# Both MLP products of a hybrid decoder layer by one level of Strassen

## The chip, the cores and the metric

The kernel runs on one core of a Trainium2 chip. The metric is the device time of one execution in microseconds (us): the median of the runs shown, lower is better. The core has five engines that matter here: TensorE (PE; its weight loads are listed apart as PEld), VectorE (DVE), ScalarE (ACT), GpSimd (POOL) and SyncE (SP), which issues most transfers. Matrix products read SBUF and write to PSUM.

## What is computed

One decoder layer over 512 tokens of 1024 features, all in float32: a gated merge of a convolution branch and a latent attention branch, a cross-attention to 256 memory tokens, an MLP and a last RMS norm. The change is in the MLP and in what feeds and follows it:

```
u = rms_norm(h, norm_mlp_g)                               # h: 512 x 1024
h = h + square(relu(u @ w_mlp1)) @ w_mlp2                 # 1024 x 4096, 4096 x 1024
return rms_norm(h, final_norm_g)
```

The two MLP products are of 512 x 1024 x 4096 multiplications each.

## The kernel before

Every float32 product runs as three passes over operands that are split into a high part (rounded to float32r, 12 significant bits) and a low part (the rest): `mm3` (lines 228 to 235) issues high x high, high x low and low x high into one PSUM bank. So each operand is first split: ACT casts the high part (line 199), and DVE or POOL subtracts it from the source for the low part (line 200, `split`; its last argument chooses the engine).

Activations are kept feature-major: feature on the partitions, 512 tokens on the free side. In a product the weights are the stationary operand (128 x 128 each) and 512 tokens move past them, so a product instruction is 128x512.

Weights lie in HBM in the order of use, in chunks of mostly 1 MB (`_stream`, line 97). `raw` (line 291) loads them from SP's queue into two buffers, one chunk ahead. `prep` (line 313) splits 1024 columns of a chunk at a time into `wh` and `wl` (three buffers each, `whl`, line 308). `Pipe.unit` (line 337) emits the splits of one unit ahead of the products of the unit before it, so that TensorE finds its weights ready. TensorE's order is that of emission; the order on the other engines is chosen by the scheduler of the framework, near the order of emission.

`w_eng` (line 321) names the engine of the low parts of the weights. In most of the first half it is POOL (line 627), while DVE runs the convolution with its running sum in PSUM. From the output projection of the cross-attention on (line 1131) it is DVE, and POOL has nothing to do until the end.

The stages that the change touches, in order:

- `xo_unit` (line 1119): the output projection of the cross-attention, in four units of two feature blocks. Behind each block `Norm.add` (line 963) adds the product to the residual `ht`, scales it by the norm's gain, splits it into `hgh` and `hgl`, and adds up its squares.
- The first MLP product, `m1_unit` (line 1151), 32 blocks of 128 hidden features in two halves of 16, each a sum over 8 blocks of input features (24 product instructions). `evac_m1` (line 1142) applies the norm's factor, relu and square and splits the result into `hh` and `hl_`.
- The second MLP product, `m2_unit` (line 1163): behind each half of the hidden features, 8 blocks of output features, each a sum over 16 hidden blocks, added to `ht`. In the second half the squares of the final norm are added up beside it.
- The last output block goes by halves of 256 tokens (lines 1189 to 1263), so that the final norm of the first half of the tokens runs beside the products of the second; then eight blocks are scaled and stored, feature-major; the host transposes the result.

Of the kernel before, what the change touches and what calls it, by code (L numbers as in the profile page):

```python
# [14 lines left out]
F32 = mybir.dt.float32  # L15
# [77 lines left out]
# gate chunks that come before the key/value latents  # L93
# [3 lines left out]
def _stream():  # L97
    """The weight chunks in the order of use: key, matrix, first row, row blocks, columns."""
# [34 lines left out]
    for h in range(2):  # L133
        for i in range(8):
            out.append((("m1", h, i), "w_mlp1", 0, 8, r(2048 * h + 256 * i, 256)))
        for i in range(8):
            out.append((("m2", h, i), "w_mlp2", 16 * h, 16, r(128 * i, 128)))
    return out


def _pack(arrays):
    """All weight chunks, each [partition, row block, column], one after the other."""
    parts = []
    for _, name, k0, kt, cols in _stream():
# [21 lines left out]
def _body(tc, a):  # L166
# [30 lines left out]
    # ---------------------------------------------------------------- exact splits and products  # L197
# [8 lines left out]
    # PE issues in the order of emission; small products that wait for other engines are put off  # L206
    # by a number of ticks (a tick: three passes over 512 columns)
# [20 lines left out]
    def mm3(out, pairs, first=True, last=True):  # L228
        n = len(pairs)
        cols = out.shape[-1] / S  # L230
        for i, ((wh, wl), (ah, al)) in enumerate(pairs):
            pe.matmul(out, wh, ah, start=first and i == 0, stop=False)  # L232
            pe.matmul(out, wh, al, start=False, stop=False)  # L233
            pe.matmul(out, wl, ah, start=False, stop=last and i == n - 1)  # L234
            tick(cols)
# [11 lines left out]
    # ---------------------------------------------------------------- constants  # L247
# [31 lines left out]
    # ---------------------------------------------------------------- weight stream  # L279
    stream = _stream()  # L280
    ch, offs = {}, []
    o = 0
    for i, (key, _, _, kt, cols) in enumerate(stream):
        ch[key] = i
        offs.append(o)
        o += P * kt * len(cols)
# [26 lines left out]
    def prep(key, k0=0, kt=None, c0=0, cols=128):  # L313
        """hi/lo of rows blocks k0.. and columns c0.. of a chunk, as [P, kt, cols]."""
# [11 lines left out]
    class Pipe:  # L326
        """splits the weights of one unit ahead of the unit before it."""
# [22 lines left out]
    # ================================================================ scopes of the first half  # L350
# [34 lines left out]
    # ---------------------------------------------------------------- x * g, split  # L385
    # the tables of the scalar engine and the clock of the PE array come up while the first loads run
# [34 lines left out]
    # ---------------------------------------------------------------- rotary tables  # L421
# [50 lines left out]
    # ---------------------------------------------------------------- background conv work  # L472
# [14 lines left out]
    def conv_gen():  # L487
        # two channel tiles in turn, so that no step waits for the one before it
# [16 lines left out]
    def layer_norm_in():  # L505
        # token-major
# [47 lines left out]
    # ---------------------------------------------------------------- w_in  # L554
# [41 lines left out]
    # first pair of channel tiles: both products follow the arriving row blocks of x  # L596
# [39 lines left out]
    # latent projections, token-major: [token, column]  # L636
# [94 lines left out]
    # ================================================================ MLA  # L731
# [148 lines left out]
    # ================================================================ merge and w_out  # L880
# [73 lines left out]
    class Norm:  # L954
        """h += psum; h * g, split; the sums of squares of h's rows."""
# [63 lines left out]
    # ================================================================ memory cross-attention  # L1019
# [3 lines left out]
    xoh = xa.tile([P, XH, S], F32R, name="xoh")  # L1023
    xol = xa.tile([P, XH, S], F32R, name="xol")
# [92 lines left out]
    n2 = Norm(hgp, "norm_mlp_g", hgh, hgl)  # L1117
# [12 lines left out]

    w_eng[0] = dve
    for m2 in range(4):
        xo_unit(m2)
    pipe.ahead(lambda: prep(("m1", 0, 0)))
    close(xa_cm, xm_cm)

    # ================================================================ MLP
    ml_cm, mlp = pool("mlp", side="right")
    hh = mlp.tile([P, 16, S], F32R, name="hh")
    hl_ = mlp.tile([P, 16, S], F32R, name="hl")  # L1140

    def evac_m1(b, m):
        t = mlp.tile([P, S], F32, tag="mz", name="mz", bufs=2)
        dve.scalar_tensor_tensor(t, b, 0.0, n2.rb, op0=ALU.max, op1=ALU.mult)  # L1144
        s = mlp.tile([P, S], F32, tag="ms", name="ms", bufs=2)
        act.activation(s, t, AF.Square)
        if m == 0:
            act.activation(warm, s[:, 0:1], AF.Sqrt)
        split(hh[:, m, :], hl_[:, m, :], s)

    def m1_unit(half, m):
        def main(hl):
            b = bank()
            mm3(b, hg_pairs(hl))
            n2.then(lambda: evac_m1(b, m))
        pipe.unit(lambda: prep(("m1", half, m // 2), c0=128 * (m % 2)), main)

    fin = mlp.tile([P, S], F32, name="fin")
    eps = mlp.tile([P, 1], F32, name="eps")
    gps.memset(eps, EPS)  # L1160
    mb_ = {}

    def m2_unit(half, m, q):
        def main(hl):
            if q == 0:
                mb_[0] = bank()
            b = mb_[0]
            mm3(b, [(lhs(hl, k), (hh[:, 8 * q + k, :], hl_[:, 8 * q + k, :])) for k in range(8)],
                first=q == 0, last=q == 1)
            if q == 1:  # L1170
                dve.tensor_tensor(ht[:, m, :], ht[:, m, :], b, op=ALU.add)
                if half == 1:
                    if m == 0:
                        act.activation(fin, ht[:, m, :], AF.Square)
                    else:
# [6 lines left out]
    for half in range(2):  # L1182
        for m in range(16):
            m1_unit(half, m)
# [104 lines left out]
```

## Time and profile before

| | us |
|---|---|
| median of 3 runs | 813.68 |
| lowest and highest | 813.56, 814.76 |
| the profiled execution: span from first to last instruction | 811.6 |
| TensorE busy in it (97% of the span) | 783.2 |
| VectorE busy (61%) | 495.9 |
| ScalarE busy (43%) | 346.4 |
| GpSimd busy (20%) | 158.6 |

The profile is of one execution; 2.1 us of the median lie outside its span. Rows of a timeline give the start, the recorded duration, the engine, the line, the operation, what is written from what is read, the shapes and the count of the instructions merged into the row; a bracket tells how long the engine had been idle and who ended that. Durations of matrix products overlap, so their pace is read from their starts. The recorded time of an instruction includes time in which it has been issued and is held. In a windows view each engine has its busy time and its number of instructions in the stretch, then follow the granted clock of TensorE (1.00 is 2.4 GHz, 0.50 is 1.2 GHz), the share of the DMA engines and GB/s.

### The profile page before, as it was taken

Reading aid. Unit: us, or ns where it says so; the run is one execution under the profiler, and the core shown is the slowest. Engines: PE = TensorE matmul, PEld = TensorE weight load, DVE = VectorE, ACT = ScalarE, POOL = GpSimd, SP = SyncE. Lnnn points to the kernel's source line nnn. Section 1 sums busy time; section 2 is a strip of 40 time slices with the busy share of each in tenths; the row PEclk is TensorE's granted clock in tenths of the full one; section 3 lists DMA queues with packets and bytes.
Section 4 is the critical chain, followed back from the end, with each engine's and each line's share of the span. In section 5 each row is a group of like instructions: output and inputs, shape, how many; then the busy total and the mean of one; then the engine's idle time right before and its main releaser. Section 6 shows DMA issues by size and latency. Waiting matters only on the chain.

```text
span 811.6 us, 9532 instructions
## 1 busy us (share of the span) xinstructions
PE 783.2 (97%) x3730; PEld 647.3 (80%) x3730; DVE 495.9 (61%) x781; ACT 346.4 (43%) x585; POOL 158.6 (20%) x92
## 2 busy tenths in 40 slices
PE   8799999999999998998999999999999999999995
PEld 4589788778788886888878888888888888888885
DVE  5898999734888869766787654443233444533333
ACT  7323334478666546343475354332212434432321
POOL 4444436322321304445320000000000000000001
PEclk9999999999999998999999999999999999999998
DMA  8213124122103242232321322222332222222203
GB/s 274 95 45 124 55 82 156 62 81 92 53 1 105 98 162 104 103 105 104 105 104 52 105 104 104 86 79 96 103 104 104 104 96 76 89 103 104 104 0 104
DMA packets 18492, 77.67 MB, mean 96 GB/s; under 512 B 1680, under 2 KB 7184, under 8 KB 11024
## 3 DMA queue, kind: packets, MB, share of 16 engines
q1 hardware_dynamic: 15120, 72.00, 25.6%
q10 hardware_dynamic: 3328, 5.07, 1.8%
q8 instruction: 29, 0.48, 0.2%
q14 instruction: 15, 0.12, 0.1%
HBM read 74.97 MB, written 2.10 MB: 95 GB/s over the span
## 4 chain that ended last, share of the span: by engine, by line
PE 75%; DVE 18%; ACT 3%; issue 3%; DMA 1%; SPq 0%; DVEq 0%; ACTq 0%
PE mm L234 23%; PE mm L232 23%; PE mm L233 23%; DVE cv L483 6%; DVE q L200 1%; DVE mt L906 1%; DVE rs_t L243 1%; DMA xr<-xT 1%; PE at L799 1%; DVE sg L710 1%; PE at L778 1%; PE at L780 1%; ACT wh L199 1%; PE at L781 0%; DVE mt L905 0%
## 5 line engine op out<-in xcount | busy, mean ns | idle before, releaser
L199 ACT CAST wh<-raw 128x1024 fp32r<-128x1024 f32 (+4 forms) x135 | 136.5, 1012 | 321.5 <-PE mm L233 279.7
L200 POOL TENSOR_TENSOR wl<-raw,wh 128x1024 fp32r<-128x1024 f32 (+4 forms) x65 | 144.6, 2227 | 255.2 <-ACT wh L199 248.1
L200 DVE TENSOR_TENSOR wl<-raw,wh 128x1024 fp32r<-128x1024 f32 x70 | 85.7, 1224 | 73.3 <-ACT wh L199 73.3
L232 PE MATMUL mm<-hgh,wh 128*128 128x512 f32 x288 | 113.0, 392 | 0.0
L234 PE MATMUL mm<-hgh,wl 128*128 128x512 f32 x288 | 112.8, 392 | 0.0
L233 PE MATMUL mm<-hgl,wh 128*128 128x512 f32 x288 | 112.6, 391 | 0.0
L232 PE MATMUL mm<-hh,wh 128*128 128x512 f32 (+1 forms) x272 | 102.6, 377 | 0.0
L233 PE MATMUL mm<-hl,wh 128*128 128x512 f32 (+1 forms) x272 | 102.4, 376 | 0.0
L234 PE MATMUL mm<-hh,wl 128*128 128x512 f32 (+1 forms) x272 | 102.4, 376 | 0.0
L483 DVE SCALAR_TENSOR_TENSOR cv<-zpad,vec,cv 128x512 f32<-128x512 f32 x116 | 80.0, 744 | 0.1
L1245 POOL TENSOR_TENSOR ht<-ht,rbf 128x256 f32<-128x256 f32 x4 | 2.9, 736 | 384.1 <-ACT rbf L1237 384.1
L232 PE MATMUL mm<-uh,wh 128*128 128x512 f32 x176 | 71.3, 405 | 1.8 <-DVE sg L710 1.8
L1144 DVE SCALAR_TENSOR_TENSOR mz<-mm,rb 128x512 f32<-128x512 f32 x32 | 22.0, 691 | 79.7 <-PE mm L234 78.7
L234 PE MATMUL mm<-uh,wl 128*128 128x512 f32 x176 | 69.8, 397 | 0.5 <-DVE wl L200 0.5
L233 PE MATMUL mm<-ul,wh 128*128 128x512 f32 x176 | 69.9, 397 | 0.0
L234 PEld LDWEIGHTS mm<-hgh,wl 128*128 128x128 f32 x288 | 54.3, 189 | 11.5
L233 PEld LDWEIGHTS mm<-hgl,wh 128*128 128x128 f32 x288 | 54.5, 189 | 11.2
L232 PEld LDWEIGHTS mm<-hgh,wh 128*128 128x128 f32 x288 | 54.5, 189 | 11.2
L234 PEld LDWEIGHTS mm<-hh,wl 128*128 128x128 f32 x272 | 51.2, 188 | 9.4
L232 PEld LDWEIGHTS mm<-hh,wh 128*128 128x128 f32 x272 | 51.2, 188 | 9.4
L233 PEld LDWEIGHTS mm<-hl,wh 128*128 128x128 f32 x272 | 51.2, 188 | 9.3
L232 PEld LDWEIGHTS mm<-uh,wh 128*128 128x128 f32 x176 | 33.3, 189 | 11.1 <-issue 3.8
(327 smaller groups left out, 1407.1 us busy)
## 6 DMA issues: line engine op xcount, KB each, us to landing
raw<-weights SPq DMA_DIRECT2D x58, 1024.0 KB, 4.8
raw<-weights SPq DMA_DIRECT2D x4, 768.0 KB, 4.2
xr<-xT SPq DMA_DIRECT2D x8, 256.0 KB, 6.2
raw<-weights SPq DMA_DIRECT2D x4, 512.0 KB, 5.1
ht<-xT ACTq DMA_DIRECT2D x1, 2048.0 KB, 9.4
raw<-weights SPq DMA_DIRECT2D x2, 576.0 KB, 3.4
mr<-memT ACTq DMA_DIRECT2D x1, 1024.0 KB, 5.8
mtok<-mem ACTq DMA_DIRECT2D x1, 1024.0 KB, 7.9
```

The costliest lines, as they stand in the source:

```text
L199: act.copy(hi, src)
L200: (eng or dve).tensor_tensor(lo, src, hi.bitcast(F32), op=ALU.subtract)
L232: pe.matmul(out, wh, ah, start=first and i == 0, stop=False)
L233: pe.matmul(out, wh, al, start=False, stop=False)
L234: pe.matmul(out, wl, ah, start=False, stop=last and i == n - 1)
L243: dve.scalar_tensor_tensor(t, dst, -0.5, dst, op0=ALU.mult, op1=ALU.mult)
L483: dve.scalar_tensor_tensor(run if w < CW - 1 else acc[:, c, :], zs, wcol, run, op0=ALU.mult, op1=ALU.add)
L710: dve.tensor_tensor(t, b, rbx, op=ALU.mult)
L778: pe.matmul(b[:, :n], q[:, 0, sl], k[:, 0, :n], start=True, stop=False)
L780: pe.matmul(b[:, :n], q[:, 0, sl], k[:, 1, :n], start=False, stop=False)
L799: pe.transpose(b[:, (t - k) * P:(t - k + 1) * P], ptok[h, t][:, k * P:(k + 1) * P], ident)
L1144: dve.scalar_tensor_tensor(t, b, 0.0, n2.rb, op0=ALU.max, op1=ALU.mult)
```

## The change

Both matrices of a product are halved in each direction, and seven products of half-size blocks (the Winograd form of Strassen's scheme) take the place of eight. Sums and differences of blocks are made before and after.

**The first product** stays feature-major. The tokens are halved (256 each), so its product instructions are 128x256. A unit is two neighbouring blocks of hidden features (16 units, 7 block products of 4 x 3 instructions each). The blocks of the activations and their four combinations are made once, in `NormS.add`, in the place of `Norm.add`, partly on POOL. The combinations of the weights are made in each unit (`prep_m1`): five on POOL, in place, and four splits of 512 or 1024 elements on ACT and DVE. The norm's factor is no longer applied here: squared, it moves behind the second product (`r2`). Hidden features are kept unsplit (`hid`). PSUM banks of a unit are accumulated again after they have been read (`again=True`).

**The second product** is token-major: hidden tokens are the stationary operand, and 512 columns of the weights move (128x512). It runs in six passes over the four chunks of a block of the weights, the third pass with two products per chunk. Each chunk splits 1024 hidden values (`split_h`, DVE for the low part) and 2048 weights (`split_w`, the low part in two POOL instructions), behind the sums that it needs (`sums_of`, `x_minus`, DVE). Blocks of the weights that are needed again are loaded again: 24 chunks instead of 16.

**The residual** is transposed by TensorE and written to HBM during the first product (`spill`), and read back token-major from ACT's queue where a result is finished (`residual`). The final norm works on rows of tokens, so that the transposes and broadcasts of the old ending go, and the output is stored token-major. A fourth buffer pair for split weights (`whl4`) is added.

The diff, cut to its core:

```diff
-    for h in range(2):
-        for i in range(8):
-            out.append((("m1", h, i), "w_mlp1", 0, 8, r(2048 * h + 256 * i, 256)))
-        for i in range(8):
-            out.append((("m2", h, i), "w_mlp2", 16 * h, 16, r(128 * i, 128)))
+    for i in range(16):
+        out.append((("m1", i), "w_mlp1", 0, 8, r(256 * i, 256)))
+    for p, (j, l) in enumerate(M2_READS):
+        for c in range(4):
+            out.append((("m2", p, c), "w_mlp2", 16 * j + 4 * c, 4, r(512 * l, 512)))
...
+        def add(self, m, b):
+            dve.tensor_tensor(ht[:, m, :], ht[:, m, :], b, op=ALU.add)
+            u = n2p.tile([P, S], F32, tag="u", name="u", bufs=2)
+            act.activation(u, ht[:, m, :], AF.Copy, scale=v_("norm_mlp_g", m))
+            j = m % 4
+            if m < 4:
+                dve.tensor_tensor(t1f[:, j, :], u[:, HT:], u[:, :HT], op=ALU.subtract)
+                split(b11[0][:, j, :], b11[1][:, j, :], u[:, :HT])
+                split(t1_[0][:, j, :], t1_[1][:, j, :], t1f[:, j, :])
+                gps.tensor_copy(u12[:, j, :], u[:, HT:])
+            else:
+                t = n2p.tile([P, 3, HT], F32, tag="hA" if m % 2 else "hB", name="t", bufs=2)
+                dve.tensor_tensor(t[:, 0, :], u[:, HT:], t1f[:, j, :], op=ALU.subtract)
+                gps.tensor_tensor(t[:, 1, :], u[:, HT:], u12[:, j, :], op=ALU.subtract)
+                dve.tensor_tensor(t[:, 2, :], u[:, :HT], t[:, 0, :], op=ALU.subtract)
+                split(b2_[0][:, j, :], b2_[1][:, j, :], u)
+                split(t234[0][:, j], t234[1][:, j], t)
...
+                gps.tensor_tensor(self.acc, self.acc, q, op=ALU.add)
...
+    def prep_m1(i):
+        r = raw("m1", i)
+        a11, a12 = r[:, 0:4, 0:128], r[:, 4:8, 0:128]
+        a21, a22 = r[:, 0:4, 128:256], r[:, 4:8, 128:256]
+        w0 = whl4(8, 128)
+        split(w0[0], w0[1], r[:, :, 0:128])
+        w3 = [n2p.tile([P, 4, 128], F32R, tag="a22" + x, name="a22" + x, bufs=2) for x in "hl"]
+        split(w3[0], w3[1], a22)
+        gps.tensor_tensor(a12, a12, a22, op=ALU.subtract)
+        gps.tensor_tensor(a22, a21, a22, op=ALU.add)
+        gps.tensor_tensor(a21, a11, a21, op=ALU.subtract)
+        gps.tensor_tensor(a11, a22, a11, op=ALU.subtract)
+        w1 = whl4(4, 256)
+        split(w1[0], w1[1], r[:, 0:4, :])
+        gps.tensor_tensor(a12, a12, a21, op=ALU.add)
+        w2 = whl4(4, 256)
+        split(w2[0], w2[1], r[:, 4:8, :])
...
+            prod(b, "s2", "t2", True)
+            prod(a, "a12", "b21", False)
+            u2 = add_to("u2", b, s1)
+            prod(b, "s3", "t3", False)
+            u3 = add_to("u3", b, s1)
+            prod(c, "s1", "t1", True)
+            c22 = add_to("c", c, u3)
+            prod(b, "a22", "t4", False)
+            prod(c, "s4", "b22", False)
...
+        square_relu(f1[:, HT:], c22)
+        c21 = add_to("c", b, s1)
+        square_relu(f1[:, :HT], c21)
+        c12 = add_to("c", c, u2)
+        square_relu(f0[:, HT:], c12)
...
+    def split_h(src):
+        hi = n2p.tile([P, 4, HT], F32R, tag="hA", name="hA", bufs=2)
+        lo = n2p.tile([P, 4, HT], F32R, tag="hB", name="hB", bufs=2)
+        split(hi, lo, src)
+        return hi, lo
+
+    def split_w(src):
+        out = []
+        for u in range(2):
+            w = whl4(2, S)
+            split(w[0], w[1], src[:, 2 * u:2 * u + 2, :], gps)
+            out.append(w)
+        return out
...
+    def x_minus(c, r, keep=None):
+        x = m2w["x"][c]
+        for u in range(2):
+            k = slice(2 * u, 2 * u + 2)
+            dve.tensor_tensor(x[:, k], r[:, k], x[:, k], op=ALU.subtract)
+        return x
...
+    def pass2(c):
+        def prep_():
+            r = raw("m2", 1, c)
+            return split_h(sums_of(c, 1)), split_w(x_minus(c, r))
...
+            chunk(acc_["c"], *hw, c)
...
+                    y = big("y11")
+                    stt(y, acc_["b"][t], r2(2 + t), keep["g", t])
+                    y_done(2 + t, 0, y)
+                    r = factors(2 + t)
+                    x = keep["y", 2 + t, 1]
+                    act.activation(x, x, AF.Copy, scale=r[:, 0:1])
+                    put(2 + t, 1, x, act.dma_start)
+                    dve.scalar_tensor_tensor(y, y, r[:, 0:1], m2w["gf"][:, :S], op0=ALU.mult,
+                                             op1=ALU.mult)
+                    put(2 + t, 0, y)
```

DVE's part of a chunk differs by pass, in instructions of 1024 elements: pass 1 the low part of the hidden block, and a copy of the 2048 weights; pass 2 a sum of hidden blocks, the low part and two `x_minus`; pass 3 two sums, the low part and two `x_minus`, and for its second product one sum and the low part; pass 4 two differences of weights, a sum and the low part; pass 5 the low part; pass 6 two `x_minus` and the low part.

## Rows read from the trace of the kernel before

**Rows 1.** The page's first line.
```profile
span 811.6 us, 9532 instructions
```
**Rows 2.** Windows: stretch, length, then PE, PEld, DVE, ACT, POOL, clock, DMA.
```profile
449.87:801.76 351.89, 351.89 (x1611) 293.55 (x1609) 141.28 (x176) 116.32 (x151) 1.44 (x2) 1.00 0.26 90
801.76:811.60 9.84, 1.17 (x8) 0.71 (x6) 3.37 (x12) 1.05 (x3) 1.42 (x2) 0.75 0.55 182
202.00:206.00 4.00, 2.58 (x16) 2.03 (x15) 3.21 (x3) 1.97 (x3) 3.61 (x2) 1.00 0.00 0
809.00:811.60 2.60, 0.00 (x0) 0.00 (x0) 0.00 (x0) 0.00 (x0) 0.00 (x0) 0.50 0.47 156
```
**Rows 3.** Timeline of PE, first and last of 46 products of 512 columns.
```profile
534.72 0.39 PE L234 MATMUL mm<-hgh,wl 128*128 128x512 f32 x1
...
544.92 0.39 PE L234 MATMUL mm<-hh,wl 128*128 128x512 f32 x1
```
**Rows 4.** Timeline of PE, first and last of 48 products of 256 columns.
```profile
788.59 0.28 PE L232 MATMUL mm<-hh,wh 128*128 128x256 f32 x1
...
794.22 0.28 PE L234 MATMUL mm<-hh,wl 128*128 128x256 f32 x1
```
**Rows 5.** Timelines of DVE and POOL from 245.85.
```profile
245.85 0.68 DVE L752 TENSOR_TENSOR qtmp<-mm,tq 128x512 f32<-128x512 f32 x1
247.48 2.48 DVE L200 TENSOR_TENSOR q<-qtmp,q 128x512 fp32r<-128x512 f32 x1 [0.95 <-ACT q L199]
...
247.01 2.39 POOL L200 TENSOR_TENSOR wl<-raw,wh 128x1024 fp32r<-128x1024 f32 x1 [3.88 <-PE at L799]
```
**Rows 6.** Timelines of DVE and POOL from 302.88.
```profile
303.69 4.96 DVE L906 TENSOR_TENSOR mt<-mt,gates 128x512 f32<-128x512 f32 x2
...
302.88 5.21 POOL L200 TENSOR_TENSOR wl<-raw,wh 128x1024 fp32r<-128x1024 f32 x2 [20.20 <-ACT wh L199]
```
**Rows 7.** Timelines of DVE and POOL from 13.47.
```profile
13.47 5.84 DVE L204 SCALAR_TENSOR_TENSOR ul<-xr,vec,uh 128x512 fp32r<-128x512 f32 x4
...
19.83 1.21 DVE L200 TENSOR_TENSOR wl<-raw,wh 128x1024 fp32r<-128x1024 f32 x1
20.97 1.78 DVE L568 TENSOR_TENSOR xr<-xr 128x512 f32<-128x512 f32 x1
...
13.91 1.45 POOL L200 TENSOR_TENSOR wl<-raw,wh 128x512 fp32r<-128x512 f32 x1 [0.91 <-ACT wh L199]
15.32 3.44 POOL L568 TENSOR_TENSOR xr<-xr 128x512 f32<-128x512 f32 x2
```
**Rows 8.** Timelines of POOL and DVE from 24.98.
```profile
24.98 4.84 POOL L200 TENSOR_TENSOR wl<-raw,wh 128x1024 fp32r<-128x1024 f32 x2
...
25.09 4.90 DVE L433 TENSOR_SCALAR ang<-kon,posf 128x16 f32<-128x16 f32 x4
```
**Rows 9.** Timeline of PE: ten transposes of 128 x 128.
```profile
213.84 1.25 PE L799 MATMUL at<-kon,p 128*128 128x128 f32 x10
```
**Rows 10.** Groups by form: DVE scales 512 elements in SBUF.
```profile
L789 DVE TENSOR_SCALAR p<-p,rl 128x512 f32<-128x512 f32 x8 | 3.9, 486 | 0.3
```
**Rows 11.** Groups by form: busy, mean ns | idle before and its releaser.
```profile
L200 DVE TENSOR_TENSOR wl<-raw,wh 128x1024 fp32r<-128x1024 f32 x70 | 85.7, 1224 | 73.3 <-ACT wh L199 73.3
...
L199 ACT CAST wh<-raw 128x1024 fp32r<-128x1024 f32 x119 | 124.9, 1051 | 294.7 <-PE mm L233 261.2 <-issue 20.4 <-PE mm L234 13.0
```
**Rows 12.** DMA issues: count, KB each, median us to landing.
```profile
raw<-weights SPq DMA_DIRECT2D x58, 1024.0 KB, 4.8
```
**Rows 13.** Timeline of DVE behind the last product.
```profile
801.96 0.42 DVE L1207 TENSOR_TENSOR ht<-ht,mm 128x256 f32<-128x256 f32 x1 [0.33 <-PE mm L234]
...
803.52 0.16 DVE L1225 TENSOR_SCALAR rv<-at 128x2 f32<-128x2 f32 x1 [1.15 <-PE at L1218]
...
804.60 0.16 DVE L1230 SCALAR_TENSOR_TENSOR rr<-rv,rr 128x2 f32<-128x2 f32 x1
```
**Rows 14.** Timeline of DVE: the first additions of the output projection.
```profile
433.07 1.37 DVE L964 TENSOR_TENSOR ht<-ht,mm 128x512 f32<-128x512 f32 x2 [3.45 <-PE mm L234]
```

More of the change, by code (lines that the diff above doesn't have):

```diff
@@ L226, in _body, with mm3 @@
     bg = lambda w: None
-    def mm3(out, pairs, first=True, last=True):
+    def mm3(out, pairs, first=True, last=True, again=False):
         n = len(pairs)
@@ L231, in mm3 @@
         for i, ((wh, wl), (ah, al)) in enumerate(pairs):
[L232 to L234 removed]
+            kw = dict(skip_group_check=True) if again else {}
+            pe.matmul(out, wh, ah, start=first and i == 0, stop=False, **kw)
+            pe.matmul(out, wh, al, start=False, stop=False, **kw)
+            pe.matmul(out, wl, ah, start=False, stop=last and i == n - 1, **kw)
             tick(cols)
@@ new lines, in m1_unit, with spill @@
+    def m1_unit(i):
+        pipe.unit(lambda: prep_m1(i), lambda w: m1_main(i, w))
+    sp_cm, spp = pool("spill", space=bass.MemoryType.DRAM)
+    hsp = spp.tile([S, D], F32, name="hsp")
+    def spill(m):
+        b = bank("at")
+        for t in range(NT):
+            pe.transpose(b[:, t * P:(t + 1) * P], ht[:, m, t * P:(t + 1) * P], ident)
+        t_ = n2p.tile([P, NT, P], F32, tag="u", name="sp", bufs=2)
+        act.copy(t_.rearrange("p t c -> p (t c)"), b)
+        act.dma_start(out=hsp[:, m * P:(m + 1) * P].rearrange("(t p) c -> p t c", p=P), in_=t_)
@@ L1151, in m1_unit @@
[L1151 to L1175, printed above, removed]
-                        s = mlp.tile([P, S], F32, tag="ms", name="ms", bufs=2)
-                        act.activation(s, ht[:, m, :], AF.Square)
-                        dve.tensor_tensor(fin, fin, s, op=ALU.add)
-                    act.activation(ht[:, m, :], ht[:, m, :], AF.Copy, scale=v_("final_norm_g", m))
-        pipe.unit(lambda: prep(("m2", half, m), k0=8 * q, kt=8), main)
@@ L1204, in last_add @@
-    def last_add(b, hf):
-        sl = slice(hf * HS, hf * HS + HS)
-        dve.tensor_tensor(ht[:, m, sl], ht[:, m, sl], b[:, :HS], op=ALU.add)
-        s = mlp.tile([P, HS], F32, tag="msl", name="msl", bufs=2)
-        act.activation(s, ht[:, m, sl], AF.Square)
-        return s
-    sb = {}
-    def last_sums(hf, sq, last):
-        if not last:
-            sb[hf] = bank("at")
-        for t in range(2):
-            pe.matmul(sb[hf][:, t:t + 1], sq[:, t * P:(t + 1) * P], ones1, start=not last and t == 0,
-                      stop=last and t == 1)
@@ new lines, in split_h, with chunk @@
+    def split_h(src):
[10 more added lines that the diff above has]
+        return out
+    def chunk(out, h, w, c, again=False, by_tile=False):
+        order = [(k, t) for t in range(2) for k in range(4)] if by_tile else \
+                [(k, t) for k in range(4) for t in range(2)]
+        for k, t in order:
+            sl = slice(t * P, (t + 1) * P)
+            mm3(out[t], [((h[0][:, k, sl], h[1][:, k, sl]), lhs(w[k // 2], k % 2, 0, S))],
+                first=not again and c == 0 and k == 0, last=c == 3 and k == 3, again=again)
@@ L1248, in _body, with put @@
[L1248 to L1264 removed]
+    def put(t, l, y, eng=None):
+        (eng or dma)(out=a["y"][t * P:(t + 1) * P, l * S:(l + 1) * S], in_=y)
@@ new lines, in r2, with stt, pass1, main @@
+    def r2(t):
+        return n2.r2[:, t:t + 1]
+    def stt(dst, x, f, y):
+        dve.scalar_tensor_tensor(dst, x, f, y, op0=ALU.mult, op1=ALU.add)
+    def pass1(c):
+        def main(hw):
+            h, w, r = hw
+            if c == 0:
+                acc_["a"] = [bank(), bank()]
+            chunk(acc_["a"], h, w, c)
+            if c == 0:
+                late_pools()
+            dve.tensor_copy(m2w["x"][c], r)
+            if c == 3:
+                for t in range(2):
+                    keep["s1", t] = big("s1")
+                    act.copy(keep["s1", t], acc_["a"][t])
+        pipe.unit(lambda: p1_prep(c), main)
@@ new lines, in pass4, with prep_, main @@
+    def pass4(c):
+        def prep_():
+            r = raw("m2", 3, c)
+            x = m2w["x"][c]
+            for u in range(2):
+                k = slice(2 * u, 2 * u + 2)
+                dve.tensor_tensor(r[:, k], x[:, k], r[:, k], op=ALU.subtract)
+            return split_h(sums_of(c, 3)), split_w(r)
+        def main(hw):
+            chunk(acc_["b"], *hw, c, True)
+            if c == 3:
+                for t in range(2):
+                    u3 = big("u2")
+                    dve.tensor_tensor(u3, acc_["b"][t], keep["s1", t], op=ALU.add)
+                    y = big("y22")
+                    dve.tensor_tensor(u3, u3, keep["s5", t], op=ALU.add)
+                    stt(y, u3, r2(2 + t), residual(2 + t, 1))
+                    y_done(2 + t, 1, y)
+                    dve.tensor_tensor(y, y, m2w["gf"][:, S:], op=ALU.mult)
+                    keep["y", 2 + t, 1] = y
+        pipe.unit(prep_, main)
```

327 lines of the change are left out of this document (249 added, 78 removed).

## The prediction

> **What bounds the kernel now.** Times are in us of the profiled execution: its span is 811.6 [rows 1], and the median of the runs shown is 813.68, 2.1 above it; that 2.1 is added at the end. I read first the windows view of the two MLP products, from the first product of one to the last of the other. From 449.87 to 801.76 TensorE is busy for all 351.89 of 351.89 at granted clock 1.00, while VectorE (DVE) has 141, ScalarE (ACT) 116 and GpSimd (POOL) 1.4 [rows 2]: the stage is bound by TensorE alone, and three engines have slack. Behind it 9.84 remain for the final norm and the stores [rows 2].
>
> Second, the timeline of TensorE, for the price of a product. The recorded durations overlap, so I take starts: 46 products of 512 columns start between 534.72 and 544.92 [rows 3], 45 steps of 0.2267. 48 products of 256 columns start between 788.59 and 794.22 [rows 4], 47 steps of 0.1198. So half the columns cost 0.53 of the time, not 0.5: narrow products give back some of what Strassen saves.
>
> Third, the timelines of DVE and POOL in the first half of the kernel, where POOL worked. At 247.01 POOL subtracts for 2.39; a DVE subtraction whose two inputs both lie in SBUF starts at 247.48 and is recorded for 2.48, so it ends at 249.96, 0.56 behind POOL's end, although its 512 elements need only about that [rows 5]. The DVE instruction before it, which reads one input from PSUM, took 0.68. In the pair at 302.88 the two engines take turns: POOL, DVE, POOL, DVE [rows 6]. The stretch from 13.47 is full: four DVE instructions of 512 elements (5.84) beside three POOL instructions of 512 (from 13.91 to 18.76) [rows 7]. One engine works and the other waits, so the durations add: 4 x 0.56 + 3 x p = 5.84 gives p = 1.20 for POOL on 512. From the pair, 2p + 0.56 = 5.21 gives p = 2.33 on 1024 [rows 6]. DVE instructions of one SBUF input are held too: four tiny ones (16 elements) took 4.90 beside two POOL instructions of 4.84 [rows 8]. I call this the shared path.
>
> **The change, part by part.** TensorE, first product: 768 products of 512 columns, 768 x 0.2267 = 174.1, become 16 units x 7 x 12 = 1344 of 256 columns, x 0.1198 = 161.0: -13.1. Second product: 720 x 0.2267 + 96 x 0.1198 = 174.7 become 7 x 4 x 24 = 672 x 0.2267 = 152.3: -22.4. The eight spills of the residual add 32 transposes, at 1.25 for ten (the idle bit in front of the next product included) [rows 9] some 4. On TensorE the change is worth about -32.
>
> The shared path, second product. Each of 28 prepared chunks gives POOL two subtractions of 1024 (wl): 56 x 2.33 = 130.5. DVE's instructions with two SBUF inputs of 1024 are, per chunk, 1 in pass 1, 4 in pass 2, 5 and 2 in the two parts of pass 3, then 4, 1 and 3: 20, times 4 = 80. Queued behind each other they start 1.14 apart (19.83 to 20.97) [rows 7]: 91.2. Pass 1 copies four raw chunks of 2048 elements; no such copy is in the trace. The nearest row scales 512 in 0.49 [rows 10], so at most 4 x 0.49 = 1.9, and hardly less than a subtraction of 1024, 1.14: I take 1.3, as most of a short instruction is overhead, 5.2 in all. The combinations at the ends of the passes (14 of 512 ahead of the tail) are 14 x 0.56 = 7.8. Sum 234.7, where TensorE needs 152.3: the pass is bound by the path, **+60** against 174.7. For the bounds: with 1.08 for DVE (twice the 0.54 by which 1.22 for 1024 exceeds 0.68 for 512) and 2.26 for POOL (the pair, had DVE's part been 0.68) it would be 226 (+51), with 5% of idle path 246 (+72). ACT's three casts of 1.05 a chunk [rows 11] lie beside it. The weight stream now fetches 24 chunks where it had 16; a fetch of 1 MB lands in 4.8 [rows 12], and the shortest chunk on the path (pass 5) takes 2 x 2.33 + 1.14 = 5.8, so it stays hidden, and without that cover it costs nothing below 4.8. The eight spills and eight residual loads of 256 KB are smaller and go from ACT's queue, which has a cast of 1.05 three times in 8: the same cover; SyncE's queue carries the weights alone.
>
> One rule differs in detail from the rows. The pair in [rows 6] leaves 5.21 - 2 x 2.39 = 0.43 for the DVE instruction in between, so a handover costs nothing that shows. The Trainium skill, SBUF — State Buffer, section "A bandwidth-pool intuition that's wrong (but worth ruling out)", puts about 115 ns between the end of a DVE instruction and the start of what GpSimd was kept from. By that the 56 POOL instructions would add at most 6.4 to the sum; the trace does not agree, and I leave it out.
>
> The shared path, first product. A unit gives POOL five combinations of 512, 5 x 1.20 = 6.0. No strided one is in the trace; the plain one at 13.91 is recorded at 1.45 with its wait [rows 7], and 1.20 is the price free of it. DVE has three low parts of 1024, one of 512 and three squares of 256 on the path, 3 x 1.14 + 0.56 + 3 x 0.28 = 4.8. Sum 10.8 a unit; TensorE needs 84 x 0.1198 = 10.06. Five more DVE instructions read PSUM at 0.42 (the one of 256 in [rows 13]), 2.1; they can run under POOL's work, unless they queue behind a blocked one. Three of them (u2, u3, c22) are read by DVE before TensorE may accumulate on the same bank again, with one product of 12 x 0.1198 = 1.44 for cover, and a blocked DVE instruction in front costs 1.2 + 1.1. So a unit lies between 10.8 and 12.9, or at TensorE's 10.06 were the path free; I take 11.4, nearer the floor, since the reads of PSUM mostly find POOL at work: 16 x 11.4 = 182.4, **+8** against 174.1 (bounds -9, at TensorE's pace with the transposes, and +32).
>
> The passage from the output projection to the first unit. Before, TensorE goes on without a gap at 449.87 [rows 2]. The eight blocks of the residual now each cost the path 2.7 (first four: 3 x 0.28 on DVE, 1.2 + about 0.6 on POOL) or 3.8 (last four: 0.28 + 0.28 + 0.56 + 0.84 and 0.6 + 1.2), 26; three splits of 1.14 and the first unit's 10 make 39. If all of it starts with the first addition at 433.07 [rows 14], it ends at 472, with TensorE free at 449.9 and covered for three products, 4.3: 18 late. If the unit's part is done before, nothing is lost. I take **+8**.
>
> The end. Before: 9.84 behind the last product. After: addition 0.7, square 0.7, the chain of small steps (803.52 to 804.76 here [rows 13], less its transposes), one scaling of 0.7 and the store. Both ends -3 and +3; I take 0, since the store, the longest part, stays.
>
> Sum: 60 + 8 + 8 = +76, span 888, plus 2.1: **890**.
>
> **Rivals.** (1) TensorE stays the bound. Place: the second product; price: the path's 234.7 falls away. For: every engine alone has less than TensorE (POOL 134, at 2.39 each). Against: all overlaps that I opened in [rows 5 to 8]. Then -13 - 22 + 4 = -31, some 782. The point from which it decides: the kernel gets no slower once 56 POOL instructions hold the path for 1.4 each in place of 2.33 and the first product keeps TensorE's pace. Chance 0.08.
>
> (2) TensorE's clock falls in the gaps that the path opens. TensorE would then work for 152 of 235. In the last 2.6 of the kernel, without a product, the granted clock is 0.50, the lower level of 1.2 GHz; in 202 to 206, where a held DVE instruction kept TensorE at 2.58 of 4.00, it stayed at 1.00, 2.4 GHz [rows 2]. At the lower level 672 products at 2 x 0.2267 take 304.7, +70 more: 960. The one row with like gaps speaks against it: chance 0.04. The Trainium skill, TensorE: Matmul & The Clock Gate, section "Part 1: The HAM clock gate (the "warmup" mystery)", has the clock gated to half by how busy the array has just been; the trace agrees as far as these two rows go.
>
> (3) Both cancel, with the path half open. Chance 0.02.
>
> **How the numbers follow.** Forecast 0.86, rivals as above. About 0.2% is what a measurement of this kernel can tell from no change. Slower is the forecast and rival 2, 0.86 + 0.04 = 0.90; faster is rival 1 and half of rival 3, 0.09; same the other half, 0.01. The forecast's own bounds add to +39 (51 - 9 + 0 - 3) and +125 (72 + 32 + 18 + 3), 850 to 940; as the ends of four terms will not meet, and as the path's prices could all be a little high, 840 to 935 holds some 0.93 of it, 0.8 of all cases.
>
> **What would show it.** In the profile after: POOL busy far over 200, most of it recorded waits; DVE's subtractions of 1024 in the second product at 2 to 3.5 where they were 1.22 [rows 11]; TensorE waiting for POOL's wl, some 152 of work in about 235; chunks of pass 5 near TensorE's 5.44 and those of pass 3's first part near 10.4; first-product units of 11 to 12; the starts of products still 0.1198 and 0.2267 apart where they follow each other. It is wrong if DVE and POOL run side by side at 1.2 and 2.4 with TensorE gapless.

## The result, and the profile after

The changed kernel takes 946.16 us (median of 4 runs, 945.94 to 947.38); the kernel before, beside it, 813.87 (4 runs). The ratio is 1.164, 95% interval 1.162 to 1.166. The side was right and the size was not: 890 was forecast, and 946 lies outside 840 to 935.

The page's first line gives the profiled execution's span; 2.0 lie around it, about as before [rows 1].

```profile
span 944.2 us, 11036 instructions
```

The windows view of its four last stretches: passage and first unit; the other units; second product; end (columns as in [rows 2]).

```profile
450.31:485.40 35.09, 17.51 (x96) 16.01 (x95) 32.34 (x36) 15.91 (x24) 23.51 (x16) 0.66 0.17 60
485.40:707.83 222.43, 178.69 (x1292) 175.45 (x1291) 111.94 (x186) 77.13 (x115) 97.61 (x73) 0.87 0.23 76
707.83:935.72 227.89, 179.44 (x673) 139.42 (x672) 209.04 (x123) 86.67 (x100) 162.65 (x55) 0.87 0.33 118
935.72:944.20 8.48, 0.39 (x2) 0.00 (x0) 3.60 (x12) 2.46 (x5) 0.00 (x0) 0.78 0.33 125
```

Against the working, whose sum is 811.6 + 76 = 887.6 on the span:

| | forecast | measured | difference |
|---|---|---|---|
| passage and first unit (8 + 11.4; to 485.4) | 19.4 | 35.1 | +15.7 |
| the next 14 units (14 x 11.4) | 159.6 | 212.5 | +52.9 |
| last unit, to the first product of the second | 11.4 | 9.9 | -1.5 |
| second product | 234.7 | 227.9 | -6.8 |
| end | 9.8 | 8.5 | -1.4 |
| start of the stage (+0.4), 3.1 of [rows 2] left in the sum (351.9 - 174.1 - 174.7), roundings | | | -2.3 |

So the second product, where the forecast had put 60 of its 76, came within its bounds. The first one, for which it gave +8 with the passage's +8, cost +83 (257.5 against 174.1).

**The second product** shows most of what the prediction said of it. The groups by form (busy, mean ns | idle before and its releasers); the first of them is of the whole run, the others of the second product:

```profile
L222 POOL TENSOR_TENSOR wl<-raw,wh 128x1024 fp32r<-128x1024 f32 x71 | 184.1, 2599 | 221.7 <-ACT wh L221 195.8 <-PE at L801 14.7 <-PE at L819 7.0
...
L222 POOL TENSOR_TENSOR wl<-x,wh 128x1024 fp32r<-128x1024 f32 x20 | 61.7, 3100 | 23.8 <-ACT wh L221 23.8
L1393 DVE TENSOR_TENSOR x<-raw,x 128x1024 f32<-128x1024 f32 x24 | 53.8, 2264 | 4.4 <-DMA raw<-weights 4.4
...
L222 DVE TENSOR_TENSOR hB<-hs,hA 128x1024 fp32r<-128x1024 f32 x16 | 40.6, 2535 | 3.2 <-ACT hA L221 3.2
```

DVE's subtractions of 1024 are recorded at 2.26 and 2.54 where they took 1.22 [rows 11]: one engine works, the other is held. Laid over each other, the recorded times of POOL and of the DVE instructions that read no PSUM cover 198.2 of the 200 from 720 to 920. The path is full. One sign differs: the prediction had TensorE wait for POOL's `wl`, and its longest waits of 707.8 to 935.7 (us in all, times, longest) are for DVE's low part of the hidden block:

```profile
PE mm L258 <- DVE hB L222: 21.8, 6, 7.1
PE at L258 <- DVE hB L222: 15.5, 5, 6.3
...
PE mm L257 <- POOL wl L222: 3.9, 5, 1.5
```

**The first product** looks different: there the same cover is 156 of the 200 from 500 to 700, and DVE or POOL, reads of PSUM included, cover 175. No engine and no path is full, TensorE included. The waits of 485.4 to 707.8 (us in all, times, longest) name what is late:

```profile
POOL raw L1230 <- DVE wl L222: 85.6, 10, 9.2
ACT wh L221 <- POOL raw L1233: 56.5, 10, 5.9
DVE wl L222 <- ACT wh L221: 50.5, 10, 5.5
...
PE at L256 <- DVE u L1264: 43.7, 16, 3.4
...
ACT wh L221 <- PE mm L257: 24.0, 12, 5.0
```

Each waits for the next, in a ring. One turn of it, from the timelines of the four engines:

```profile
543.78 1.05 ACT L221 CAST wh<-raw 128x1024 fp32r<-128x1024 f32 x1 [1.99 <-PE mm L257]
...
544.86 1.23 DVE L222 TENSOR_TENSOR wl<-raw,wh 128x1024 fp32r<-128x1024 f32 x1
...
546.16 1.29 POOL L1230 TENSOR_TENSOR raw<-raw 128x512 f32<-128x512 f32 x1 [8.09 <-DVE wl L222]
...
550.26 1.29 POOL L1233 TENSOR_TENSOR raw<-raw 128x512 f32<-128x512 f32 x1
...
551.58 1.04 ACT L221 CAST xh<-raw 128x1024 fp32r<-128x1024 f32 x1 [5.04 <-POOL raw L1233]
...
552.66 1.22 DVE L222 TENSOR_TENSOR xl<-raw,xh 128x1024 fp32r<-128x1024 f32 x1 [4.59 <-ACT xh L221]
553.80 0.41 DVE L1264 TENSOR_TENSOR u<-at,s 128x256 f32<-128x256 f32 x1
...
554.27 0.39 PE L256 MATMUL at<-t234h,a22h 128*128 128x256 f32 x1 [2.54 <-DVE u L1264]
...
558.82 1.05 ACT L221 CAST wh<-raw 128x1024 fp32r<-128x1024 f32 x1 [1.55 <-PE mm L257]
```

Read it downwards; the names are those of the code, and `u3` is what `add_to("u3", b, s1)` writes. ACT casts the first half of a unit's weights, DVE makes its low part, and only then may POOL write its four sums over the raw weights (546.16 to 551.55, each 1.36 behind the last). ACT casts the sums, DVE makes their low part, and behind that low part in DVE's queue stands `u3`, the read of PSUM that TensorE waits for, 0.41 long. The product that it reads had ended at about 550.1, and DVE was idle for 4.59 in front of that low part. Then 24 products run (a22 x t4, s4 x b22), the last of which frees the buffer for the next cast, 15.04 after the first.

The last leg, 554.27 to 558.82, is 4.55 for 24 products, which at [rows 4] take 2.9. The clock is why. Two pairs of rows of TensorE's timeline, each eleven products of 256 columns apart, ahead of the gap that ended at 554.27 and in the leg:

```profile
550.17 0.28 PE L256 MATMUL mm<-t1h,wh 128*128 128x256 f32 x1
...
551.45 0.28 PE L258 MATMUL mm<-t1h,wl 128*128 128x256 f32 x1
...
555.35 0.41 PE L256 MATMUL at<-t234h,a22h 128*128 128x256 f32 x1
...
557.69 0.41 PE L258 MATMUL mm<-b2h,wl 128*128 128x256 f32 x1
```

That is 0.116 a product (2.4 GHz) and 0.213 (1.2 GHz). The mean granted clock of the stretch is 0.87.

### The profile page after: what moved, and what is told of

The parts are those of the page before. It is cut to its first block, busy times and chain, and to the rows that moved or that the text cites. A ratio compares the mean times of both kernels' runs of the same rounds, so it can differ in the third digit from the quotient of the medians.

```text
span 944.2 us, 11036 instructions
## 1 busy us (share of the span) xinstructions
PE 807.0 (85%) x4170; PEld 684.4 (72%) x4170; DVE 710.2 (75%) x948; ACT 413.1 (44%) x682; POOL 450.9 (48%) x239
## 2 busy tenths in 40 slices
DMA packets 24117, 90.88 MB, mean 96 GB/s; under 512 B 2048, under 2 KB 9600, under 8 KB 15616
## 5 line engine op out<-in xcount | busy, mean ns | idle before, releaser
L222 POOL TENSOR_TENSOR wl<-raw,wh 128x1024 fp32r<-128x1024 f32 (+4 forms) x87 | 209.4, 2412 | 290.7 <-ACT wh L221 264.8
L222 POOL TENSOR_TENSOR wl<-x,wh 128x1024 fp32r<-128x1024 f32 x20 | 61.7, 3100 | 23.8 <-ACT wh L221 23.8
L258 PE MATMUL mm<-wh,hB 128*128 128x512 f32 x88 | 40.0, 455 | 21.8 <-DVE hB L222 21.8
L1393 DVE TENSOR_TENSOR x<-raw,x 128x1024 f32<-128x1024 f32 x24 | 53.8, 2264 | 4.4 <-DMA raw<-weights 4.4
L258 PE MATMUL at<-wh,hB 128*128 128x512 f32 x80 | 35.5, 444 | 19.6 <-DVE hB L222 15.5
L256 PEld LDWEIGHTS at<-t234h,a22h 128*128 128x128 f32 x64 | 16.9, 264 | 46.5 <-DVE u L1264 46.5
L222 DVE TENSOR_TENSOR hB<-hs,hA 128x1024 fp32r<-128x1024 f32 x16 | 40.6, 2535 | 3.2 <-ACT hA L221 3.2
L257 PE MATMUL mm<-wl,hA 128*128 128x512 f32 x88 | 38.6, 438 | 3.9 <-POOL wl L222 3.9
L258 PEld LDWEIGHTS mm<-uh,wl 128*128 128x128 f32 x176 | 33.3, 189 | 9.1 <-DVE wl L222 1.0
L257 PEld LDWEIGHTS mm<-ul,wh 128*128 128x128 f32 x176 | 33.5, 190 | 7.3
L256 PE MATMUL mm<-wh,hA 128*128 128x512 f32 x88 | 38.2, 434 | 0.0
```

The costliest lines, as they stand in the source:

```text
L222: (eng or dve).tensor_tensor(lo, src, hi.bitcast(F32), op=ALU.subtract)
L256: pe.matmul(out, wh, ah, start=first and i == 0, stop=False, **kw)
L257: pe.matmul(out, wh, al, start=False, stop=False, **kw)
L1393: dve.tensor_tensor(x[:, k], r[:, k], x[:, k], op=ALU.subtract)
```

## The experiments

Each is one execution of a variant, on a chip on which the kernel before took 813.5 to 814.7. "Units" are the distances of the first products of neighbouring units; in the changed kernel they are 35.1, then 13.5 to 16.2, 15.2 in the mean. Their floor on TensorE is 84 x 0.1198 = 10.1. Idle products are products into a part of PSUM that nobody reads.

### Low parts of the second product's weights from POOL to DVE

```diff
-            split(w[0], w[1], src[:, 2 * u:2 * u + 2, :], gps)
+            split(w[0], w[1], src[:, 2 * u:2 * u + 2, :])
```

> Only the low parts of the second product's weights move from POOL to DVE. Theory A (DVE and POOL take turns on the path, durations add): 136 DVE subtractions of 1024 at 1.14 plus 13 make 168 us in place of 226 to 235, so the second product takes 170 to 180 and the kernel 890 to 900 us. Rival (two engines share the work, and DVE alone is too slow for it): the second product takes 226 us or more, the kernel 946 us or more.

Measured: 897.75; second product 181.4 (227.9), first 255.5 (257.5). The windows view of the second product: DVE does what POOL did and is busy for 171 in place of 209.

```profile
706.10:887.50 181.40, 162.99 (x673) 128.27 (x672) 171.03 (x176) 88.86 (x100) 0.00 (x0) 0.96 0.42 148
```

One engine with all the work is faster than two that hold each other: the price of POOL on this path (2.33 against 1.14) was most of the loss. 46.5 came back where the two prices give 56 x 1.19 = 67 and theory A had at most 180: DVE, alone on the path, is not busy all the time.

### The second product without its sums

```diff
-            return split_h(sums_of(c, 1)), split_w(x_minus(c, r))
+            return split_h(blk(1, 0, c)), split_w(r)
```

and in the other passes alike; POOL keeps its 56 subtractions.

> The second product leaves out its sums of hidden blocks and its differences of weights (all DVE instructions of two SBUF inputs except the low parts); POOL's 56 subtractions stay. Theory A: 56 x 2.33 + 28 x 1.14 + 13 = 175 us for the second product, the kernel about 895 us. Rival (POOL alone, or the chain cast then POOL, sets the pace): at most TensorE's 152 to 155 us if POOL's 130 us are all that counts, the kernel below 875 us; or no change if the chain through POOL bounds it.

Measured: 897.8; second product 181.3. Taking 52 sums and differences of 1024 from DVE gives 46.6 back, 0.9 each where 1.14 was taken, and theory A had 175. So DVE's share of the path is worth time too, as durations that add should be, but not its full price: the path is covered for 153.9 of the 160 from 720 to 880, and ACT's casts, which had waited for weights for 3 in the changed kernel, now wait 38.9:

```profile
ACT wh L221 <- DMA raw<-weights: 38.9, 13, 6.2
```

### The first product's combinations from POOL to DVE

```diff
-        gps.tensor_tensor(a12, a12, a22, op=ALU.subtract)
+        dve.tensor_tensor(a12, a12, a22, op=ALU.subtract)
```

and the other four of a unit.

> Only the five combinations of a unit's weights in the first product move from POOL to DVE. Theory B (a chain bounds the unit: low part on DVE, four POOL combinations at 1.3, cast, low part on DVE, and only behind it the read of PSUM that TensorE waits for): four combinations of 0.6 in place of 5.4 us, so a unit takes about 12 us in place of 14.8 and the kernel about 900 us. Rival C (DVE and POOL durations add on the path here too): DVE's sum of 10.3 a unit is hardly below the 10.8 that both made, so the unit keeps at least 14 us and the kernel 930 us or more.

Measured: 882.3. Units 10.2 to 12.1, the first 28.6; first product 191.7. The stretch from the second unit on:

```profile
478.76:641.75 162.99, 155.12 (x1291) 151.69 (x1290) 150.41 (x263) 75.86 (x117) 6.68 (x3) 1.00 0.33 111
```

DVE is busy for 38 us more than in the changed kernel's stretch, and yet a unit loses 4.2 and comes within 0.9 of TensorE's floor (10.9 in the mean). Work was not what was missing. That is more than expected.

### DVE's and ACT's order in the first product by hand

The last two splits of the next unit's weights are put behind `u2`, `u3` and `c22` of the unit at work, POOL as it was.

```diff
             u3 = add_to("u3", b, s1)
             prod(c, "s1", "t1", True)
             c22 = add_to("c", c, u3)
...
+        more(i + 1)
```

> Same instructions on the same engines, but on DVE and ACT in the first product the splits of the next unit's combined weights stand behind the reads of PSUM that TensorE waits for. Theory B (the order on DVE is what costs): the unit falls from 14.8 to 10.8 to 11.5 us, the first product by 55, the kernel to about 890 us. Rival C (the path itself is full in the first product): no change, 946 us within 10.

Measured: 911.7. Most units 12.4, the first 37.3, clock 0.98 behind it. A good part of the loss is the place of `u3` in the queue; less came back than expected. What is left is a shorter ring of the same kind. The waits of 500 to 660:

```profile
ACT wh L221 <- POOL raw L1232: 71.8, 10, 7.9
POOL raw L1229 <- DVE wl L222: 55.0, 10, 6.7
```

That 12.4 is near the 12.9 of the prediction is chance: the 12.9 was for reads of PSUM that do not run under POOL's work, and here 15.6 of their 26.9 lie under POOL's sums, in the changed kernel 5.2 of 27.8 (500 to 700).

### Both moves to DVE

> Both single moves at once: the 56 subtractions of the second product and the five combinations of a unit of the first go from POOL to DVE; POOL does nothing in the two products but the norm's sums. Theory A (each product has its own cause, the filled shared path in the second, the chain over POOL in the first, and neither cover reaches over into the other): the savings add, first product with passage about 192 as in the run with the combinations on DVE, second about 181 as in the run with the low parts on DVE, kernel 946 - 48 - 64 = 834, within 4. Rival B (the end of the first product and the start of the second share DVE, so that a part of the saving is counted twice): 842 or more, and the second product over 186.

Measured: 835.2, first product 191.9, second 182.7. The two savings add; the products have causes of their own.

### Towards a faster version

Both moves; also the norm's sums on DVE, its copy and the copy of pass 1 on ACT, and the first unit's first splits ahead of the last units of the output projection.

```diff
+            if m2 == 3:
+                first[0] = prep_first(0)
...
-                gps.tensor_tensor(self.acc, self.acc, q, op=ALU.add)
+                dve.tensor_tensor(self.acc, self.acc, q, op=ALU.add)
...
-            dve.tensor_copy(m2w["x"][c], r)
+            act.copy(m2w["x"][c], r)
```

> Towards a faster version: nothing on POOL in either product, the norm's sums too on DVE and its copy on ACT; the first unit's first two splits and four combinations are emitted ahead of the last two units of the output projection; the copy of the weights in pass 1 goes to ACT. Theory A (the passage is late because the first unit's weights queue behind the eight blocks of the residual): the first unit takes 20 or less where it took 28.6 with the combinations alone on DVE, units after it 10.1 to 10.8, second product 176 to 180, kernel 818 to 826. Rival B (what fills the passage is DVE's work on the eight blocks itself, 8 x 3 or so behind 433, and no order of the weights helps): the first unit stays at 26 or more, kernel 829 or more.

Measured: 828.5; first unit 24.0, second product 180.9. Between the two theories on the passage, and still 15 slower than before. No variant beat the kernel before: with DVE alone on the path the second product stays at 181, above the 174.7 that it had without Strassen.

### Idle products in the gaps of the first product

```diff
...
             c22 = add_to("c", c, u3)
+            for _ in range(16):
+                pe.matmul(d, w["s1"][0][:, 3], t1_[0][:, 3, :], start=True, stop=True,
+                          skip_group_check=True)
             prod(b, "a22", "t4", False)
```

> The changed kernel with 16 idle products of 256 columns (into an unused half of a bank, never read) ahead of the product that waits for u3, in each of 15 units: TensorE works through 1.9 of the 2.7 that it waits there. Theory A (the first product is late because of the chain through ACT, DVE and POOL, and the low clock is only its mark): the granted clock of the first product rises from 0.87 to 0.95 or more and the units stay at 14 to 15.5, kernel 940 to 952. Rival B (the clock that falls in the gaps is itself a good part of the loss, as products at the lower level take twice as long and lie on the chain): with the clock back the units lose over 1 each, kernel 930 or less.

Measured: 923.4, units 13.2 to 15.4, most of them 13.6. The kernel has 240 products more and takes 23 us less, of which 4.2 lie ahead of the first product. But the scheduler had also moved one square of DVE's in each unit, so the clock was not shown yet. Hence the next two, with the order of DVE and ACT written out as the scheduler had given it to the changed kernel, from the second unit on; the second has the same idle products, and all engines but TensorE have the same instructions in the same order.

> The changed kernel with the order of DVE and ACT in the first product written out by hand, and the same from the second unit on as the scheduler gave it; POOL's order too. It is the base for the next run, in which TensorE alone gets more to do. Both theories: units of 14.5 to 15.6 as in the changed kernel (mean 15.1), granted clock 0.82 to 0.9, second product 228; the kernel within 6 of 946, what differs being the first unit.

> The kernel with the written-out order and the 16 idle products in 15 units ahead of the product that waits for u3; DVE, ACT and POOL have the very same instructions in the very same order. In the earlier run with idle products DVE's order had also changed in one place of each unit (a square ahead of a low part). Theory B (the low clock itself costs the time): units of 13.2 to 13.9 as there, 1.5 below the base, granted clock 0.95 or more, kernel some 20 under the base. Theory A (that gain came from the changed order): units within 0.5 of the base at a clock of 0.95 or more.

Measured: 949.7 and 932.6, the first unit 39.5 in both. Windows of the two from their second unit on, first without, then with idle products:

```profile
490.30:709.50 219.20, 174.33 (x1289) 171.13 (x1288) 110.89 (x179) 76.82 (x113) 97.55 (x73) 0.89 0.23 81
```

```profile
490.10:693.80 203.70, 183.38 (x1529) 180.14 (x1528) 109.11 (x179) 76.94 (x113) 98.84 (x74) 1.00 0.26 87
```

And TensorE's wait for `u3` from 490 to 650 in the two:

```profile
PE at L256 <- DVE u L1290: 35.0, 12, 3.7
```

```profile
PE at L256 <- DVE u L1290: 15.6, 13, 1.9
```

The 14 units behind the first sum to 209.5 without and 192.2 with; the granted clock goes from 0.89 to 1.00. The low clock alone costs 17 us, and work that nobody needs buys them back. Within the base the units of 13.2 to 13.6 have a granted clock of 1.00, those of 14.8 to 15.9 one of 0.79 to 0.89.

The Trainium skill, TensorE: Matmul & The Clock Gate, section "A second HAM failure mode: psum-queue depth-cycling", tells of a kernel whose short idle times between groups of products made the clock swing between its two levels; the trace agrees, with 0.116 and 0.213 a product within 8 us.

### Combinations that nobody waits for

POOL writes its five sums into a tile of their own.

```diff
-        gps.tensor_tensor(a12, a12, a22, op=ALU.subtract)
+        gps.tensor_tensor(x, a12, a22, op=ALU.subtract)
```

and the other four alike.

> POOL makes the five combinations of a unit into a tile that nobody reads; the splits take the raw blocks. Left out: the combinations' use, so the last two splits of a unit are of blocks of the weights as they are. The path has the same work, but no cast and no low part waits for POOL, and what stands behind them in DVE's queue is free. Theory A (the chain over POOL sets the unit, not the path's work): units of 10.8 to 12, near the 11.4 of the prediction, clock 0.97 or more, kernel 890 to 905. Rival B (the path's work sets it, held reads of PSUM included, more than the 12.9 I allowed): units of 13.5 or more, kernel 925 or more.

Measured: 899.7; the 14 units sum to 159.7, most of them 11.2 (the first unit 39.4). Windows from its second unit on:

```profile
489.09:658.43 169.34, 158.09 (x1289) 153.67 (x1288) 138.10 (x185) 76.66 (x113) 114.78 (x67) 0.99 0.30 100
```

POOL makes as many sums, DVE and ACT have the same instructions in the same order as in the changed kernel from the second unit on, and a unit takes what the prediction had put down for it: 11.4 x 14 is 159.6. So the waits, which the sum left out, made the unit late. What sets the 11.2 is not shown: the path is covered for 139.0 of the 150 from 500 to 650, and TensorE is busy for 158.1 of the 169.3.

### Idle products in the second product

```diff
+    def fill(h, w):
+        for _ in range(10):
+            pe.matmul(m2w["d"], h[0][:, 0, :P], w[0][0][:, 0, :], start=True, stop=True,
+                      skip_group_check=True)
...
+            fill(*hw)
             chunk(acc_["c"], *hw, c)
```

and ahead of three more such lines.

> Idle products in the second product instead: 10 of 512 columns ahead of each chunk of passes 2, 4 and 6 and of the first part of pass 3 (16 chunks, 2.3 each), into a bank that nobody reads; TensorE waits there 50 of 228 in the changed kernel. Theory A (the shared path sets the pace of the second product, 198 of 200 of its time taken, so the clock costs nothing there): granted clock up to 0.95 or more from 0.79 to 0.96, second product 225 to 232, kernel 943 to 951. Rival B (as in the first product, the clock is part of the loss): second product 220 or less.

Measured: 956.2; second product 237.9, 10 more, clock 0.94 instead of 0.87.

```profile
708.00:945.94 237.94, 204.58 (x833) 162.94 (x832) 189.47 (x123) 86.70 (x100) 163.47 (x55) 0.94 0.32 113
```

Neither number came: the idle products (36 us of them) did not all fit into the waits. With the clock nearly back the second product is no shorter. That, and the full path, speak for the clock being no loss here; the idle products' own time keeps it from being settled.

### Two more weight buffers

```diff
...
+            if ring[0] % 5 == 4:
+                hi = n2p.tile([P, 1024], F32R, tag="hA", name="hA", bufs=2)
+                lo = n2p.tile([P, 1024], F32R, tag="hB", name="hB", bufs=2)
```

> The changed kernel with one thing more in the first product from the second unit on: two more buffer pairs for split weights (the buffers of the hidden splits, idle then), so that a unit's first cast no longer waits for the last product of the unit before the last. Nothing is moved from POOL and nothing is left out. Theory A (the unit is one closed loop: last product frees the buffer, cast, low part, four sums on POOL, cast, low part, u3, a22 x t4, s4 x b22, which frees the next buffer, 15.0 long in the timeline): the loop is opened, units fall to 11.2 to 13, the clock comes back to 0.95 or more by itself, first product 205 to 225, kernel 895 to 920. Rival B (u3 behind the split in DVE's queue and the occupied path set the unit, the buffer is only one of several waits that end at the same time): units of 14 or more, kernel 930 or more.

Measured: 952.1; units 13.1 to 17.3. The ring as drawn above, closed by the buffer, is not what sets the unit. TensorE's waits from 490 to 700, the two longest:

```profile
PE mm L256 <- ACT s L1288: 38.5, 12, 4.6
...
PE at L256 <- DVE u L1272: 5.9, 2, 3.0
```

The wait for `u3` is nearly gone (43.7 before), and one of the same size has come in ACT's queue: there the copy `s1`, for which TensorE waits, now stands behind casts that wait for POOL; the scheduler had changed the order on ACT with the buffers. The buffer was one of several waits that end together; what stays is a cast or a low part that waits for POOL's four sums, with something short and urgent queued behind it.

## Why the prediction was wrong

- **The shared path in the second product (+60, bounds +51 to +72): right.** Measured 227.9 - 174.7 = +53.2, with 198.2 of 200 covered; the prices together were 3% high. The copy of pass 1 took 1.22 where it ran free, 1.3 taken; of the 0.49 for 512 [rows 10] that leaves, as an estimate, half that does not grow with the size, not most of it. Moving POOL's part to DVE and taking DVE's away gave 46.5 and 46.6 back. The sign "POOL busy far over 200, most of it recorded waits" came by its number alone: the page has 450.9, of which 163 lie here, 53 subtractions of 3.08 where 2.33 was the price. Most of the held time is DVE's, recorded for 209 where its prices give 104.
- **The first product's unit (11.4; 10.8 to 12.9): the step that failed.** What it put down for a unit without the waits agrees with 11.2, though 11.4 was a choice between 10.8 and 12.9 and not a sum. What failed is "they can run under POOL's work, unless they queue behind a blocked one", with the blocked one priced at 1.2 + 1.1. The instruction in front of `u3` was not held by one POOL instruction; it waited for a cast that waited for four of them, 5.4 + 1.1. Of the +53 on 14 units some 33 is this (192.2 at full clock against 159.7), and the runs that shorten the chain give it back, in part by the queue's order (12.4 a unit) or wholly with the sums on DVE (10.9).
- **Rival 2, the clock: right in kind, in the wrong stage.** It was placed in the second product, where the full path seems to hide it, with [rows 2] as the row that spoke against it. The gaps of the first product made it fall, and 17 to 20 of the +53 are its (209.5, or 212.5 in the changed kernel, against 192.2). The row from 202 to 206 was one gap; 14 units each with a gap of 2.7 were another matter.
- **The passage (+8, 0 to 18): the bound itself was too low.** The path's work on the eight blocks ended at 476.1, 4 behind the 472 that was worked out; it had served sums and low parts of the second unit by then (POOL's from 470.3 on). Behind it the bound of 18 left the unit 7.1 (11.4 less the three early products). The last blocks feed the products with t2, t3 and t4, 36 of 84, and the end of those with b2, which could only run then: that took 9.3, to 485.4, at a clock of 0.66 for the stretch. TensorE's waits ahead of that are of the kind of the units': 7.1 for a cast that stood in ACT's queue behind waits for POOL (3.9 and 1.8), 4.2 for a low part, 4.0 for the copy `s1` in ACT's queue. With the weights' sums on DVE the first unit took 28.6, with the norm's too and the weights ahead 24.0; how the rest divides between DVE's work and the clock was not tried.
- **TensorE's own saving (-13, -22): there, and worth nothing**, since no stage was left bound by TensorE; the first product came near it once its sums were on DVE. The end (0, taken as -3 to +3) came at -1.4. The cover of the weight stream held in the changed kernel: from 707.8 on DVE and ACT waited some 8 for weights, in the first product's units not at all.

TensorE's three longest waits of the passage (450.3 to 485.4):

```profile
PE mm L256 <- ACT wh L221: 7.1, 1, 7.1
PE mm L258 <- DVE wl L222: 4.2, 1, 4.2
PE mm L256 <- ACT s L1280: 4.0, 1, 4.0
```

The range failed with the unit, and by less with the passage: their bounds were those of work on the path, and no term stood for a chain of waits through four engines.

## What to carry to other kernels

Two engines on a common path are slower than one of them with all the work, if the other's price is higher. A stage where no engine is full, as the first product here, is a chain: follow the longest wait from engine to engine until it closes, and look for short instructions that stand in a queue behind long waits. Before adding gaps to a stage that TensorE bounds, price what its clock does in them; a few idle products show it, if the order on all other engines stays as it was.

## What the runs showed of the hardware that was not expected

240 idle products shortened the kernel by 17 us with all other instructions and their order alike, since the granted clock stayed at 1.00. A copy of 2048 elements on DVE, of which the kernel before had no row, takes 1.22, no longer than a subtraction of 1024 (L1473 in the run with the low parts on DVE):

```profile
L1473 DVE COPY x<-raw 128x2048 f32<-128x2048 f32 x4 | 4.9, 1223 | 0.7 <-DMA raw<-weights 0.7
```
